# Old keys and values of the sample attention: regrouped within DRAM ahead of the mixer, then loaded in 4 KB rows

## The chip, the cores and the metric

One Trainium2 chip, one of its cores. The metric is the device time of one execution in microseconds; lower is better. The kernel before takes 2782.64 us (median of 3 runs, 2779.88 to 2784.14).

## What is computed

One inference step of one decoder layer over 256 prompt tokens and 64 sample tokens (8 sequences of 8), 320 columns in all: a SwiGLU feed-forward, a token mixer (mLSTM and dilated attention), a second feed-forward, a final norm. For the change, one part of the mixer matters: the dilated attention of the sample tokens over a cache of 2048 old keys and values for each of the 8 sequences, 8 heads of 128 numbers each, so that a row of the cache is 1024 fp32 numbers (4 KB).

```python
PATTERNS = ((128, 1), (512, 4), (2048, 16))       # window, dilation

def dilated_attention_sample(q, k_all, v_all, biases):
    qi = k_all.shape[1] - T + jnp.arange(T)        # T = 8 new tokens
    for (w, d), bias in zip(PATTERNS, biases):
        idx = qi[:, None] - d * jnp.arange(w // d + 1)[None, :]
        kg = k_all[:, idc]                         # idc = clip(idx, 0)
        vg = v_all[:, idc]
        s = jnp.einsum('bthe,btjhe->bhtj', q, kg) + bias
        ...
        num = jnp.einsum('bhtj,btjhe->bthe', p, vg)
```

Beyond the last 512 positions only the third pattern is left, dilation 16: of the 1536 far rows, 8 in each group of 16 neighbours are read (one for each of the 8 new tokens), 768 rows for each sequence.

## The kernel before

Every large product is written out in one list of jobs, each with its weights in chunks of 512 x 256 fp32 numbers (512 KB). For a chunk the SyncE queue (SP) loads a `raw` buffer (5 of them), ScalarE casts it to `hi` (L225), VectorE subtracts `lo` (L226), and TensorE runs 24 matmuls (L144) of 320 columns, which give fp32 accuracy from two rounded halves. `run_job` goes from chunk to chunk; ahead of the matmuls of chunk i it splits up to chunk i + 2, steps the side work once, and issues loads up to chunk i + 7. The order of every engine is thus the order in which the program is written. The job list is feed-forward a (272 chunks), the mixer's input projection, gates, the mixer's output projections, feed-forward b.

The side work is written as generators that advance by one `yield` per chunk (`every`), per second chunk (`even`, `odd`), or eight times in fifteen chunks (`slow`). In the first part of the projection runs `sample_attention` (`slow`): 16 units, each one sequence b and four heads hg. For a unit, `load_k` brings its keys in five pieces pr into `kraw` (3 buffers) and `load_v` its values in six pieces pc into `vt` (6 buffers). Pieces 0 and 1 of each are the 512 near rows, with a DMA of 512 KB each. The others are far rows: `kraw` pieces 2 to 4 hold 256 of them in 128 partitions, two rows to a partition, `vt` pieces 2 to 5 hold 192 in 96. For four heads, half of a cache row is wanted, 2 KB; the two halves of such a buffer (index g) are filled by two DMAs of 128 or 96 rows of 2 KB. VectorE then transposes each `kraw` (L654), in line with its `lo` of the weights; TensorE takes `vt` directly. In the same stretch run the mLSTM (`odd`), which loads and stores its matrix state C, and `prompt_attention`, and most intermediate results go to DRAM and come back, all on the SP queue, in the order of the program (L141 is the helper that issues nearly every DMA). A DMA also waits until the eighth before it has landed, since the tracked semaphores are used in turn.

Of the kernel before, what the change touches and what calls it, by code (L numbers as in the profile page):

```python
# [9 lines left out]
F32 = mybir.dt.float32  # L10
# [12 lines left out]
PAST = 2048  # L23
# [105 lines left out]
def decoder_kernel(tc, I, O, K):  # L129
# [7 lines left out]
    dp = es.enter_context(tc.tile_pool(name="dp", bufs=1, space=DRAM))  # L137
    es.enter_context(tc.manual_schedule())

    def dma(out, in_):  # L140
        nc.sync.dma_start(out, in_)  # L141

    def mm(out, a, b, start=True, stop=True, **kw):
        T.matmul(out, a, b, start=start, stop=stop, **kw)  # L144

    def bcast(ap, n, at=1):
        shape = list(ap.shape)
        shape.insert(at, n)
        idx = [slice(None)] * len(ap.shape)
        idx.insert(at, None)  # L150
        return ap[tuple(idx)].to_broadcast(shape)

    def raw_ap(ap, off, dims):
        return bass.AP(tensor=ap.tensor, offset=ap.offset + off, ap=dims)
# [3 lines left out]
    def later(fn, n=1):  # L158
        later_q.append([n, fn])
# [23 lines left out]
    def spawn(g, lst=None, first=False):  # L183
        lst = every if lst is None else lst
        lst.insert(0 if first else len(lst), g)
# [68 lines left out]
    def bg_tile():  # L254
        return pp.tile([128, 512], F32, tag="bg", bufs=4, name="bg")
# [79 lines left out]
    def tr(out, in_):  # L335
        k = in_.shape[0]
        T.transpose(out, in_, ident[:k, :k])  # L337
# [14 lines left out]
    rows_d = dp.tile([4, 2, NT], F32, name="rows_d")  # L352
    sc_d = dp.tile([4, 2 * NS], F32, name="sc_d")
    sT_d = dp.tile([1, 32], F32, name="sT_d")

    XH, XL = {}, {}

# [73 lines left out]
    def load_vecs():  # L431
        for r, nm in ((16, "ln_mix"), (32, "ln_ffb"), (48, "conv_b")):
            dma(vrow[r - 16:r, 0], I[nm].rearrange("o (k p) -> (o k) p", p=128))
        dma(vrow[48:112, 0], I["conv_w"].rearrange("o i (k p) -> (o i k) p", p=128))
        dma(vrow[0:8, 1], I["m_norm"].rearrange("o (k p) -> (o k) p", p=128))
        dma(vrow[8:24, 1], I["ln_f"].rearrange("(k p) -> k p", p=128))
# [72 lines left out]
    def mxt(shape, tag, bufs, name, dt=F32):  # L509
        return M["p"].tile(shape, dt, tag=tag, bufs=bufs, name=name)  # L510
# [119 lines left out]
    def sample_attention():  # L630
        ck, cv = I["cache_k"][0], I["cache_v"][0]
# [9 lines left out]
        def load_k(u, pr):  # L641
            hg, b = divmod(u, 8)
            t = mxt([128, 2, 512], "kr", KRB, "kraw")
            off = b * PAST * 1024 + hg * 512
            if pr < 2:
                dma(t, raw_ap(ck, off + (1536 + 2 * pr) * 1024, [[4096, 128], [1024, 2], [1, 512]]))
            else:
                for g in range(2):
                    dma(t[:, g], raw_ap(ck, off + 16 * (2 * (pr - 2) + g) * 1024, [[96 * 1024, 16], [1024, 8], [1, 512]]))
            kraw[u, pr] = t  # L650

        def tk(u, pr):
# [5 lines left out]
        def load_v(u, pc):  # L658
            hg, b = divmod(u, 8)
            t = mxt([128, 2, 512], "v4", 6, "vt")  # L660
            off = b * PAST * 1024 + hg * 512
            if pc < 2:
                dma(t, raw_ap(cv, off + (1536 + 256 * pc) * 1024, [[1024, 128], [128 * 1024, 2], [1, 512]]))
            else:
                hf, gp = divmod(pc - 2, 2)
                for g in range(2):
                    dma(t[0:96, g], raw_ap(cv, off + 16 * (48 * gp + 24 * g + 12 * hf) * 1024,
                                           [[16 * 1024, 12], [1024, 8], [1, 512]]))
                if pc == 4:
                    dma(t[96:104, 0], vs_d[8 * b:8 * b + 8, hg * 512:(hg + 1) * 512])  # L670
            VT[u, pc] = t
# [14 lines left out]
        for pr in range(KRB):  # L686
            load_k(0, pr)
        yield
        for pr in range(5):
            tk(0, pr)  # L690
            load_k(*divmod(pr + KRB, 5))
            yield
# [782 lines left out]
    def last_tr(m):  # L1475
        xn, a = Y["xn"], bg_tile()
        for t, t0 in enumerate(TOK):
            tr(a[:, t * 128:(t + 1) * 128], xn[:, m, t0:t0 + 128])
        return a
# [87 lines left out]
    def first_chunk(n, ps):  # L1567
# [18 lines left out]
        wh.pop(n)  # L1586
        wl.pop(n)

    def vec_table():
        for _ in range(8):  # L1590
            yield
        load_vecs()
        for _ in range(4):
            yield
        vps = bg_tile()
        tr(vps[:, 0:112], vrow[0:112, 0])
        tr(vps[:, 112:136], vrow[0:24, 1])
        V.tensor_copy(gv[:, 16:152], vps[:, 0:136])

    def first_sumsq():  # L1600
        for c in ((), (), (), (0, 1), (2, 3), (4, 5, 6, 7)):
            for j in c:
                sumsq(X[j], j, fp)
            yield

    def init_tables():
        for _ in range(6):
            yield
        tab = fp.tile([128, TABW], F32, name="tab")
        dma(tab, K["tab"])  # L1610
        rel = fp.tile([128, 8], F32, name="rel")
        for u in range(4):
            dma(rel[32 * u:32 * u + 32], I["rel_table"])
        cst = fp.tile([24, D], F32, name="cst")
        dma(cst, I["state_conv"].rearrange("o b r c -> (o b r) c"))
        n0 = fp.tile([64, 128], F32, name="n0")
        dma(n0, I["state_n"].rearrange("o b h (k p) -> (o b h k) p", p=128))
        for _ in range(6):
            yield
        lt = fp.tile([128, 2, 3, 128], F32, name="lt")  # L1620
        for hg in range(2):
            rb = bcast(rel[:, 4 * hg:4 * hg + 4], 32, 2)
            for kt in range(3):
                G.tensor_tensor(lt[:, hg, kt].rearrange("p (h c) -> p h c", h=4), rb,
                                bcast(tab[:, T_DL + 32 * kt:T_DL + 32 * kt + 32], 4), op=OP.mult)
        sr = fp.tile([8, RW], F32, name="sr")
        ps, pb = bg_tile(), bg_tile()
        for c0, q in ((0, ps), (RW // 2, pb)):
            mm(q[0:8, 0:RW // 2], rel[0:32], tab[0:32, T_OHR + c0:T_OHR + c0 + RW // 2])
            V.tensor_copy(sr[:, c0:c0 + RW // 2], q[0:8, 0:RW // 2])  # L1630
        yield
        dma(srev_d, sr)
        yield
        yield
        sb = fp.tile([128, 2, 128], F32, name="sb")
        for t in range(8):
            for hg in range(2):
                dma(sb[t:128:8, hg], raw_ap(srev_d[:], 4 * hg * RW + 7 - t, [[RW, 4], [128, 4], [1, 128]]))
            yield
        for hg in range(2):  # L1640
            ps = bg_tile()
            mm(ps[:, 128:320], lt[:, hg, 0], tab[:, T_OHO:T_OHO + 192])
            for kt in range(2):
                mm(ps[:, 320:328], lt[:, hg, 1 + kt], tab[:, T_OHN + 8 * kt:T_OHN + 8 * kt + 8], kt == 0, kt == 1)
            V.tensor_tensor(ttab[:, hg, 0:128], sb[:, hg], tab[:, T_MK:T_MK + 128], op=OP.add)
            V.tensor_tensor(ttab[:, hg, 128:SCOLS], ps[:, 128:SCOLS], tab[:, T_MK + 128:T_MK + SCOLS], op=OP.add)
            yield
        ps = bg_tile()
        mm(ps[0:8, 0:384], rel[0:32], tab[0:32, T_OHP:T_OHP + 384])
        gs = fp.tile([8, 384], F32, name="gs")  # L1650
        V.tensor_tensor(gs, ps[0:8, 0:384], tab[0:8, T_MKP:T_MKP + 384], op=OP.add)
        yield
        dma(grev_d, gs)
        flip = fp.tile([128, 128], F32, name="flip")
        dma(flip, K["flip"])
        ps = bg_tile()
        for k in range(16):
            tr(ps[:, 24 * k:24 * k + 24], cst[:, k * 128:(k + 1) * 128])
        V.tensor_copy(convst, ps[:, 0:384].rearrange("p (k c) -> p k c", k=16))
        yield  # L1660
        ps = bg_tile()
        tr(ps[:, 0:64], n0)
        V.tensor_copy(n0T, ps[:, 0:64])
        for p in range(4):
            tw = fp.tile([128, 3, 512], F32, tag="xl", bufs=3, name="tw")
            tf, to = tw[:, 0], tw[:, 1]
            dma(tf.rearrange("p (a c) -> p a c", a=2), raw_ap(grev_d[:], 2 * p * 384, [[1, 128], [384, 2], [1, 256]]))
            yield
            ps = bg_tile()
            mm(ps, flip, tf)  # L1670
            V.tensor_copy(to, ps)
            later(lambda to=to, p=p: dma(tp_d[p], to), 2)

    spawn(first_sumsq())
    spawn(vec_table())
    spawn(init_tables(), even)
    for job in jobs[:-1]:
        run_job(job)
# [5 lines left out]
    a = last_tr(1)  # L1684
# [56 lines left out]
```

## Time and profile before

| | |
|---|---|
| median of 3 runs | 2782.64 us |
| the profiled execution | 2780.48 us, of it 2778.7 us span |
| TensorE busy | 2727.4 us, 98% of the span |
| VectorE, ScalarE busy | 1534.0 us, 1104.3 us |
| DMA | 557.22 MB, 201 GB/s over the span |
| mean granted TensorE clock | 0.993 |

The span is the time from the first instruction to the last. Feed-forward a runs from 60 to 897 us, the projection with the attention and the mLSTM beside it to about 1630, the gates and output projections to 1903, feed-forward b to the end.

### The profile page before, as it was taken

The page shows a single profiled execution, that of the slowest core. Times are in us where ns is not written, and L with a number is a line of the kernel's source. Part 1 is how long each engine was busy: PE and PEld are TensorE (multiplying, and loading weights), DVE is VectorE, ACT ScalarE, POOL GpSimd, SP SyncE. Part 2 cuts the span into 40 slices and gives each one's busy share as a digit, 9 for nine tenths or more (in the row PEclk, how much of TensorE's full clock was granted, in tenths as well). Part 3 has the DMA queues.
Part 4 walks back from the last instruction along what each step waited for, and adds up shares of the span by engine and source line. Part 5 has one row for each costly group of instructions (what it writes and reads, how often), then busy time and mean ns, then how long its engine had stood idle before and what let it go on. Part 6 is the DMA issues. An engine that isn't in the chain of part 4 may idle for free.

```text
span 2778.7 us, 51128 instructions
## 1 busy us (share of the span) xinstructions
PE 2727.4 (98%) x21522; PEld 2678.3 (96%) x21522; DVE 1534.0 (55%) x1815; ACT 1104.3 (40%) x1379; POOL 179.5 (6%) x226
## 2 busy tenths in 40 slices
PE   9999999999999999998999999999999999999998
PEld 8999999999999999987989899999999999999998
DVE  6444444444447656776766565755444444444444
ACT  5333333333335333544543434544333333333344
POOL 0100000000000000111211100000000000000000
PEclk9999999999999999999999999999999999999999
DMA  6555555555556789999999997655555555545543
GB/s 213 163 160 179 160 162 164 160 157 163 166 155 206 213 218 301 288 290 265 308 307 304 320 302 251 205 184 170 161 164 159 163 160 167 159 152 174 160 152 114
DMA packets 507763, 557.22 MB, mean 201 GB/s; under 512 B 30156, under 2 KB 452604, under 8 KB 507508
## 3 DMA queue, kind: packets, MB, share of 16 engines
q1 hardware_dynamic: 506828, 552.43, 65.4%
q8 instruction: 168, 2.75, 0.4%
q10 hardware_dynamic: 704, 1.52, 0.2%
q14 instruction: 63, 0.52, 0.1%
HBM read 521.58 MB, written 32.28 MB: 199 GB/s over the span
## 4 chain that ended last, share of the span: by engine, by line
PE 86%; DMA 9%; DVE 3%; ACT 1%; issue 1%; POOLq 0%; POOL 0%; SPq 0%; ACTq 0%; DVEq 0%
PE fg L144 82%; DMA raw<-in_w_in_dram 4%; PE bg L144 3%; DMA kraw<-in_cache_k_dram 2%; PE bg L337 1%; DVE lo L226 1%; DMA vt<-in_cache_v_dram 1%; ACT hi L225 0%; DVE kd L654 0%; DMA out_C_sample_dram<-C 0%; DMA vh<-vm_d 0%; DMA out_conv_sample_dram<-cs 0%; DVE y L947 0%; DMA vq<-vm_d 0%; DMA mo_d<-sg 0%
## 5 line engine op out<-in xcount | busy, mean ns | idle before, releaser
L226 DVE TENSOR_TENSOR lo<-raw,hi 128x1024 fp32r<-128x1024 f32 (+1 forms) x780 | 956.9, 1234 | 894.0 <-ACT hi L225 876.9
L144 PE MATMUL fg<-xh,hi 128*128 128x320 f32 x4240 | 1277.6, 302 | 1.7 <-ACT hi L225 1.6
L144 PE MATMUL fg<-xh,lo 128*128 128x320 f32 x4240 | 1267.8, 300 | 10.9 <-DVE lo L226 10.9
L144 PE MATMUL fg<-xl,hi 128*128 128x320 f32 x4240 | 1267.3, 300 | 0.0
L225 ACT CAST hi<-raw 128x1024 fp32r<-128x1024 f32 (+1 forms) x780 | 796.8, 1027 | 1092.4 <-PE fg L144 912.0
L144 PEld LDWEIGHTS fg<-xh,lo 128*128 128x128 f32 x4240 | 802.1, 189 | 12.9 <-DVE lo L226 12.8
L144 PEld LDWEIGHTS fg<-xh,hi 128*128 128x128 f32 x4240 | 802.3, 190 | 4.1 <-ACT hi L225 2.1
L144 PEld LDWEIGHTS fg<-xl,hi 128*128 128x128 f32 x4240 | 802.4, 190 | 0.7
L144 PE MATMUL fg<-hh,hi 128*128 128x320 f32 x1408 | 423.7, 301 | 0.0
L144 PE MATMUL fg<-hl,hi 128*128 128x320 f32 x1408 | 421.0, 299 | 0.0
L144 PE MATMUL fg<-hh,lo 128*128 128x320 f32 x1408 | 421.0, 299 | 0.0
L144 PEld LDWEIGHTS fg<-hh,hi 128*128 128x128 f32 x1408 | 266.1, 189 | 1.7 <-issue 1.6
L144 PEld LDWEIGHTS fg<-hl,hi 128*128 128x128 f32 x1408 | 266.1, 189 | 1.0 <-issue 1.0
L144 PEld LDWEIGHTS fg<-hh,lo 128*128 128x128 f32 x1408 | 266.1, 189 | 0.0
L464 POOL TENSOR_TENSOR gt<-gt,rstd 128x640 f32<-128x640 f32 x44 | 68.3, 1552 | 1788.8 <-ACT gt L463 1788.8
L144 PE MATMUL fg<-bh,hi 128*128 128x320 f32 x512 | 153.3, 299 | 0.0
L144 PE MATMUL fg<-bl,hi 128*128 128x320 f32 x512 | 153.1, 299 | 0.0
L144 PE MATMUL fg<-bh,lo 128*128 128x320 f32 x512 | 153.1, 299 | 0.0
L654 DVE STREAM_TRANSPOSE kd<-kraw 128x1024 f32<-128x1024 f32 x80 | 96.5, 1220 | 32.5 <-DMA kraw<-in_cache_k_dram 32.5
L144 PEld LDWEIGHTS fg<-bh,hi 128*128 128x128 f32 x512 | 96.8, 189 | 0.2 <-issue 0.2
L144 PEld LDWEIGHTS fg<-bl,hi 128*128 128x128 f32 x512 | 96.8, 189 | 0.0
L144 PEld LDWEIGHTS fg<-bh,lo 128*128 128x128 f32 x512 | 96.8, 189 | 0.0
(301 smaller groups left out, 1375.7 us busy)
## 6 DMA issues: line engine op xcount, KB each, us to landing
raw<-in_w_in_dram SPq DMA_DIRECT2D x176, 512.0 KB
raw<-in_w_ffb_in_dram SPq DMA_DIRECT2D x176, 512.0 KB
raw<-in_w_ffa_in_dram SPq DMA_DIRECT2D x175, 512.0 KB
raw<-in_w_ffa_out_dram SPq DMA_DIRECT2D x80, 512.0 KB
raw<-in_w_ffb_out_dram SPq DMA_DIRECT2D x80, 512.0 KB
kraw<-in_cache_k_dram SPq DMA_DIRECT2D x96, 256.0 KB
vt<-in_cache_v_dram SPq DMA_DIRECT2D x128, 192.0 KB
kraw<-in_cache_k_dram SPq DMA_DIRECT2D x32, 512.0 KB
```

The source lines that it names most:

```text
L144: T.matmul(out, a, b, start=start, stop=stop, **kw)
L225: S.copy(hi[:, :nk], t[:, :nk])
L226: V.tensor_tensor(lo[:, :nk], t[:, :nk], hi[:, :nk].bitcast(F32), op=OP.subtract)
L337: T.transpose(out, in_, ident[:k, :k])
L464: G.tensor_tensor(gt, gt, bcast(rstd, 2), op=OP.mult)
L654: V.transpose(kd[:, 2 * pr:2 * pr + 2].rearrange("p a b -> p (a b)"), t.rearrange("p a b -> p (a b)"))
```

## The change

During feed-forward a, a new generator `gather_old` copies the far rows of all units from the cache into two new sets of DRAM tensors, `fk_d` and `fv_d`, one DMA for each chunk: 16 units with 6 copies of keys (128 rows of 2 KB) and 8 of values (96 rows), 224 copies. It skips its first ten steps. In the copy, the two rows that share a partition stand side by side. In the mixer, each far piece is one DMA with 4 KB for each partition instead of two with 2 KB: 112 loads where 224 were. Arithmetic, buffers and the near loads are as before.

```diff
+    fk_d = [dp.tile([3, 128, 1024], F32, name=f"fk_d{u}") for u in range(16)]
+    fv_d = [dp.tile([4, 96, 1024], F32, name=f"fv_d{u}") for u in range(16)]
...
@@ load_k
-                for g in range(2):
-                    dma(t[:, g], raw_ap(ck, off + 16 * (2 * (pr - 2) + g) * 1024, [[96 * 1024, 16], [1024, 8], [1, 512]]))
+                dma(t, fk_d[u][pr - 2].rearrange("p (a c) -> p a c", a=2))
...
@@ load_v
-                hf, gp = divmod(pc - 2, 2)
-                for g in range(2):
-                    dma(t[0:96, g], raw_ap(cv, off + 16 * (48 * gp + 24 * g + 12 * hf) * 1024,
-                                           [[16 * 1024, 12], [1024, 8], [1, 512]]))
+                dma(t[0:96], fv_d[u][pc - 2].rearrange("p (a c) -> p a c", a=2))
...
+    def gather_old():
+        ck, cv = I["cache_k"][0], I["cache_v"][0]
+        for _ in range(10):
+            yield
+        for u in range(16):
+            hg, b = divmod(u, 8)
+            off = b * PAST * 1024 + hg * 512
+            for i in range(3):
+                for g in range(2):
+                    dma(fk_d[u][i].rearrange("(x r) (g c) -> x r g c", r=8, g=2)[:, :, g],
+                        raw_ap(ck, off + 16 * (2 * i + g) * 1024, [[96 * 1024, 16], [1024, 8], [1, 512]]))
+                    yield
+            for i in range(4):
+                hf, gp = divmod(i, 2)
+                for g in range(2):
+                    dma(fv_d[u][i].rearrange("(x r) (g c) -> x r g c", r=8, g=2)[:, :, g],
+                        raw_ap(cv, off + 16 * (48 * gp + 24 * g + 12 * hf) * 1024, [[16 * 1024, 12], [1024, 8], [1, 512]]))
+                    yield
...
     spawn(vec_table())
+    spawn(gather_old())
```

TensorE, VectorE, ScalarE and GpSimd execute the same instructions in the same order before and after. Only the SP queue changes, in two stretches. The first is feed-forward a, near its twentieth chunk: loads of constants (`cst`, `n`), then loads of weights (`raw`). On SP stood there:

```order
L141 DMA cst<-in_state_conv_dram 24x2048
L141 DMA n_729<-in_state_n_dram 64x128
L141 DMA raw<-in_w_ffa_in_dram 128x4x256 x14
L141 DMA srev_d<-sr 8x520
L141 DMA raw<-in_w_ffa_in_dram 128x4x256 x4
```

And now stand there, with the copies of the first unit's keys (`fk_d_96`):

```order
L141 DMA cst<-in_state_conv_dram 24x2048
L141 DMA n_763<-in_state_n_dram 64x128
L141 DMA fk_d_96<-in_cache_k_dram 128x1x512
L141 DMA raw<-in_w_ffa_in_dram 128x4x256
L141 DMA fk_d_96<-in_cache_k_dram 128x1x512
L141 DMA raw<-in_w_ffa_in_dram 128x4x256
```

Each load of weights has one copy ahead of it, from the eleventh step to the 234th of the 272 of this feed-forward.

The second stretch is the mixer. In the eighth unit of the attention, far values (`vt`) stand on SP between weights, results of the mLSTM (`out_C_prompt`, `out_C_sample`) and near keys, as a piece of the difference:

```order
 L141 DMA raw<-in_w_in_dram 128x4x256
 L141 DMA out_C_prompt_dram<-cn 128x2x256
-L141 DMA vt<-in_cache_v_dram 96x1x512 x2
-L141 DMA raw<-in_w_in_dram 128x4x256
-L141 DMA vt<-in_cache_v_dram 96x1x512 x2
+L141 DMA vt<-fv_d_119 96x1024
+L141 DMA raw<-in_w_in_dram 128x4x256
+L141 DMA vt<-fv_d_119 96x1024
 L141 DMA out_C_sample_dram<-C 128x2x256
 L141 DMA kraw<-in_cache_k_dram 128x2x512
```

Two loads of 2 KB rows became one of 4 KB rows, in the same place. A few rows later on SP the same is seen with far keys (`kraw`):

```order
 L141 DMA raw<-in_w_in_dram 128x4x256
 L141 DMA out_C_sample_dram<-C 128x2x256
-L141 DMA kraw<-in_cache_k_dram 128x1x512 x2
+L141 DMA kraw<-fk_d_105 128x1024
 L141 DMA raw<-in_w_in_dram 128x4x256 x2
 L141 DMA out_C_sample_dram<-C 128x2x256
```

Nothing but the pair moved; the weights behind it stand one issue nearer.

## Rows read from the trace of the kernel before

**Rows 1.** Page, busy time by engine; then TensorE and DMA in 40 slices.

```profile
PE 2727.4 (98%) x21522; PEld 2678.3 (96%) x21522; DVE 1534.0 (55%) x1815; ACT 1104.3 (40%) x1379; POOL 179.5 (6%) x226
...
DMA  6555555555556789999999997655555555545543
```

**Rows 2.** Windows by stage: stretch, its length, busy time, granted clock, DMA share, GB/s.

```profile
core 0: us, PE busy (x) PEld busy (x) DVE busy (x) ACT busy (x) POOL busy (x), PEclk, DMA share, GB/s
60.00:770.00 710.00, 710.00 (x5206) 705.73 (x5205) 341.39 (x312) 249.84 (x256) 33.54 (x25) 1.00 0.54 165
1000.00:1200.00 200.00, 197.01 (x1913) 189.89 (x1911) 136.11 (x242) 80.79 (x139) 17.68 (x30) 1.00 1.00 282
1200.00:1300.00 100.00, 92.65 (x900) 85.11 (x901) 71.81 (x125) 44.48 (x69) 19.16 (x38) 0.97 0.94 277
1300.00:1400.00 100.00, 90.20 (x834) 83.25 (x833) 68.87 (x116) 52.48 (x80) 20.11 (x29) 0.95 1.02 303
1400.00:1500.00 100.00, 93.95 (x868) 86.53 (x867) 69.62 (x102) 42.48 (x68) 17.49 (x33) 0.97 1.02 312
1500.00:1630.00 130.00, 124.03 (x1200) 116.28 (x1199) 82.89 (x122) 49.70 (x76) 19.84 (x27) 0.97 1.02 310
1630.00:1903.00 273.00, 273.00 (x2182) 270.94 (x2181) 163.41 (x181) 124.63 (x152) 0.00 (x0) 1.00 0.69 220
```

**Rows 3.** Waits, 1000 to 1630 us: who waited for whom, us, times, longest.

```profile
ACT hi L225 <- DMA raw<-in_w_in_dram: 59.7, 15, 9.0
DVE kd L654 <- DMA kraw<-in_cache_k_dram: 32.5, 9, 7.9
PE fg L144 <- DVE lo L226: 9.5, 4, 5.5
PE bg L144 <- DVE lo L226: 6.4, 1, 6.4
PE bg L144 <- DMA vh<-vm_d: 6.0, 1, 6.0
```

**Rows 4.** Chain that ended last, 1260 to 1345 us: start, us, what.

```profile
1257.52 9.15 DMA kraw<-in_cache_k_dram
...
1273.93 12.44 DMA raw<-in_w_in_dram
```

**Rows 5.** Waits of the SP queue itself, 1000 to 1630 us; then 232 to 897 us.

```profile
SPq L141 <- DMA raw<-in_w_in_dram: 108.9, 85, 2.9
SPq L141 <- DMA vt<-in_cache_v_dram: 48.8, 90, 1.8
SPq L141 <- DMA kraw<-in_cache_k_dram: 27.2, 51, 1.8
...
SPq L141 <- DVE lo L226: 566.3, 211, 5.0
```

**Rows 6.** Page, issues of far keys and of far values: count, KB each.

```profile
kraw<-in_cache_k_dram SPq DMA_DIRECT2D x96, 256.0 KB
vt<-in_cache_v_dram SPq DMA_DIRECT2D x128, 192.0 KB
```

**Rows 7.** DMA, 300 to 500 us, weights alone: packets, MB, share of 16 engines.

```profile
DMA packets 32401, 32.37 MB, mean 162 GB/s; under 512 B 992, under 2 KB 32386, under 8 KB 32386
q1 hardware_dynamic: 32386, 32.15, 52.2%
```

**Rows 8.** DMA, 938 to 939 us, while near keys arrive.

```profile
DMA packets 234, 0.41 MB, mean 406 GB/s; under 512 B 13, under 2 KB 59, under 8 KB 234
q1 hardware_dynamic: 234, 0.41, 105.8%
```

**Rows 9.** DMA, 1000 to 1630 us.

```profile
DMA packets 147805, 185.77 MB, mean 295 GB/s; under 512 B 12531, under 2 KB 105662, under 8 KB 147740
q1 hardware_dynamic: 147740, 184.87, 99.5%
```

**Rows 10.** DMA, 2771 to 2778.7 us: the output, stored with 4 KB a packet.

```profile
DMA packets 594, 2.07 MB, mean 269 GB/s; under 512 B 89, under 2 KB 89, under 8 KB 594
q1 hardware_dynamic: 313, 1.05, 47.3%
q10 hardware_dynamic: 281, 1.02, 34.3%
```

**Rows 11.** SP's issues: `kraw`, `vt` overall; `raw` 232 to 897 us (ns min/median/max).

```profile
L141 SPq DMA_DIRECT2D kraw<-in_cache_k_dram x128: 367/582/1381, 908.3 to 1632.7; - x128
L141 SPq DMA_DIRECT2D vt<-in_cache_v_dram x160: 368/810/2170, 1006.4 to 1677.8; - x160
L141 SPq DMA_DIRECT2D raw<-in_w_ffa_in_dram x128: 367/368/368, 244.8 to 804.0; - x128
```

## Prediction

> **What bounds the kernel now.** First the page: TensorE is busy 98% of the span, and the DMA row stands at five or six tenths except in one stretch in the middle, where it stands at nine [rows 1]. So I asked for windows by stage [rows 2]. In feed-forward a (60 to 770 us) TensorE has no idle microsecond and DMA is 0.54 busy; from 1630 on TensorE is full again. Between lies the only place where time is lost: 2.99 us idle in 1000 to 1200, then 7.35, 9.80, 6.05 and 5.97 us in the four windows to 1630, together 32.2 us. In the same four windows the granted clock falls to 0.95 to 0.97, which costs up to 0.03 x 100 + 0.05 x 100 + 0.03 x 100 + 0.03 x 130 = 15 us more; part of the low clock lies inside the idle time, so I count 12. The ceiling for a change that acts on the mixer alone is thus about 44 us, 1.6% of the whole, and since TensorE is full behind it, what is won there moves the end by as much.
>
> What makes TensorE wait? In that stretch all 16 DMA engines are busy (0.94 to 1.02). The waits [rows 3] show the way it takes: VectorE stands 32.5 us before the transposes of `kraw`, ScalarE 59.7 us before casts of `raw`, and TensorE then waits for `lo`, which stands behind these in VectorE's order (9.5 + 6.4 us), or for a DMA itself. The chain agrees [rows 4]: links of 9 and 12 us from the issue of a load to its landing. The SP queue shows the backlog from the other side: 108.9 + 48.8 + 27.2 = 185 us it waits for the landing of earlier DMAs, while in feed-forward a it waits for `lo` alone, which means for a free buffer [rows 5]. So the mixer is bound by DMA, or near it; feed-forward a is bound by TensorE with DMA to spare.
>
> **What the far loads cost, and what they will.** There are 96 loads of 128 rows and 128 loads of 96 rows [rows 6], 12,288 + 12,288 = 24,576 packets of 2 KB, between 1006 and 1678 us [rows 11]. The price of a packet comes from stretches with known mixtures. Weights alone: 52.2% of 16 engines over 200 us is 1670 us for 32,386 packets, 51.6 ns for 1 KB [rows 7]. Near keys in a quiet microsecond: 16.9 us of engine time, less 46 packets of 1 KB, leaves 14.5 us for 175 packets, 83 ns for 2 KB [rows 8]. In the mixer: 99.5% of 16 x 630 is 10,030 us; 93,131 packets of 1 KB take 4,806 of it, 12,531 small ones between nothing and 650, so the 42,078 of 2 KB and a little more take 109 to 124 ns each [rows 9]. I take 117. The far loads then hold the 16 engines for 24,576 x 0.117 / 16 = 180 us.
>
> After the change there are 12,288 packets of 4 KB. No row shows such a load. The nearest are the stores of the output: 281 packets of the second queue in 34.3% of 7.7 us, 42.3 us, of which 249 would be 4 KB, 170 ns; both queues together 100.5 us for 505 packets, 199 ns [rows 10]. From below stand two quiet packets of 2 KB, 166 ns; from above two of the mixer's, 234 ns, which would be no gain. I take 180, near the stores, because the new rows are contiguous as theirs are: 12,288 x 0.180 / 16 = 138 us. The gain is 42 us of DMA time over the 672 us, 6.2% (0 at 234 ns; 9% at 166 against 124).
>
> Half the issues of far loads go too: 48 of `kraw` at a median 0.58 us and 64 of `vt` at 0.81 us, 80 us of SP's time in the mixer [rows 11]. SP is in order, so weights that stand behind a pair are issued sooner; and each DMA that SP waits for is larger, so that the same number in flight covers more bytes. I give this no sum of its own: it is what could turn the 6.2% into more.
>
> What it gives TensorE: from 1200 to 1630 the stage goes at the pace of DMA, so 6.2% of 430 us is 27 us, of 29 us idle and 12 us of clock lost there. In 1000 to 1200 only 3 us are lost, and I count 1 of it. Sum: 28 us.
>
> **What the copies cost in feed-forward a.** A step there is 24 of 5206 matmuls in 710 us, 3.27 us [rows 2]. The weights of a step are 512 packets, 32 for each engine, 32 x 51.6 ns = 1.65 us; 1.62 us are left. A copy adds 128 or 96 packets, on average (6 x 8 + 8 x 6) / 14 = 6.9 for each engine. No row shows a copy from DRAM to DRAM. Bounds: as cheap as a quiet load, 83 ns; as dear as two of the mixer's packets one after the other, 234 ns. Between them I take a quiet read and a quiet write in turn, 166 ns, since feed-forward a is nearer to the quiet rows than to the mixer: 1.14 us, and the step needs 2.79 of 3.27 us. It breaks even at 1.62 / 6.9 = 235 ns, just at the upper bound. The cover is five `raw` buffers and idle DMA; if it is gone, each 10 ns beyond costs 0.069 x 224 = 15 us, and the next thing late is `raw` for the cast, then TensorE. SP has room for 224 more issues: it waits 566 of 665 us for buffers [rows 5], and an issue takes 0.37 us [rows 11]. A copy waits for nothing but the landing of the eighth DMA before it, four steps ago, and the weights behind it in the queue wait for a buffer anyway. The last copy is issued some 38 steps, 120 us, before the mixer reads the first, so that the new dependence costs nothing. I cost feed-forward a at nothing.
>
> [...]
>
> **Sum.** 2780.5 us of the profiled execution, less 28, is 2752.5. That execution is 2.1 us under the median of the runs, 2782.6; with half of that I say 2753.
>
> **Rivals.** *Full relief* (chance 0.18): fewer issues and larger DMAs in flight do more than the share says, or 4 KB costs 166 ns. For it speak the 185 us that SP waits for landings; against it, that some loads stand behind others' results (`vh` from `vm_d`), which keep their way through DRAM. 2780 - 40 = 2740.
>
> *The row size buys nothing* (0.14): a packet costs by its bytes, 4 KB is 2 x 117, and TensorE's waits come from bursts rather than the mean. For it speaks that quiet prices are proportional beyond a few ns (83 for 2 KB, 170 for 4 KB), so all the gain lies in the mixer's surcharge of 34 ns, which I cannot tie to the far rows; in 1000 to 1200 DMA stands at 1.00 and TensorE loses only 1.5%. Then 2775 to 2786. [...]
>
> *Feed-forward a becomes bound by DMA* (0.22): a copy reads and writes the same DRAM from which the weights stream, and a packet passes 235 ns. At 270 ns: 0.035 x 6.9 x 224 = 54 us lost, 28 won, 2806; at 300 ns 2852. For it speaks that the upper bound is already at break-even; against it, that DMA is idle 46% of that time and that a single copy stands between weights, never two.
>
> **Chances and range.** The forecast, 15 to 36 us less, has 0.46; full relief 0.18, nothing 0.14, the loss 0.22. The two first make it faster, and a little of the third: 0.66. Within 0.2% (5.6 us, about what a measurement of this kernel can tell from no change): 0.14. Slower: 0.20. Its own range is 2744 to 2768; since cases of both signs hold much, I give 2738 to 2804, which leaves out the far end of the loss and a gain near the ceiling.
>
> **What would show it.** Right: feed-forward a keeps TensorE at 100% with a DMA share near 0.8; in 1200 to 1630 the share falls under 1.00 or the stage becomes shorter by some 27 us; the waits of VectorE for `kraw` shrink most; packets of 4 KB cost 170 to 190 ns. Wrong: idle TensorE behind `lo` between 60 and 770 us, with SP waiting there for landings rather than for `lo`; or an unchanged wait for `raw` and `kraw` in the mixer although DMA has become less busy, which would mean that bursts and order, not the mean load, set it.

## The result and the profile after

The changed kernel takes 2747.25 us (median of 4 runs, 2745.51 to 2749.30), beside 2781.57 us of the kernel before (median of 4 runs here, the profiled one among them): 34.3 us less, and a ratio of 0.9886 (95% interval 0.9871 to 0.9900). The forecast was 2753 us, within 2738 to 2804.

The profiled execution took 2745.51 us, its span 2743.7. The windows of the changed kernel by stage, with the columns of [rows 2]; the mixer's part that had ended at 1630 us now ends at about 1595:

```profile
core 0: us, PE busy (x) PEld busy (x) DVE busy (x) ACT busy (x) POOL busy (x), PEclk, DMA share, GB/s
60.00:770.00 710.00, 710.00 (x5206) 705.73 (x5205) 341.35 (x312) 250.12 (x256) 33.53 (x25) 1.00 0.74 234
1000.00:1200.00 200.00, 200.00 (x1977) 192.78 (x1976) 141.21 (x260) 82.61 (x141) 17.39 (x30) 1.00 1.00 296
1200.00:1300.00 100.00, 94.94 (x886) 88.38 (x885) 76.44 (x128) 52.59 (x81) 19.76 (x38) 0.97 0.95 294
1300.00:1400.00 100.00, 96.50 (x916) 90.56 (x916) 81.05 (x128) 52.90 (x83) 26.64 (x41) 1.00 1.03 331
1400.00:1500.00 100.00, 98.89 (x928) 92.62 (x927) 68.52 (x97) 44.47 (x69) 17.62 (x28) 1.00 1.05 333
1500.00:1600.00 100.00, 100.00 (x1042) 93.42 (x1041) 66.11 (x96) 41.16 (x63) 14.73 (x18) 1.00 1.02 322
...
1595.00:1870.00 275.00, 275.00 (x2196) 272.83 (x2195) 164.61 (x182) 126.76 (x153) 0.00 (x0) 1.00 0.70 220
```

Three things are to be seen. Feed-forward a is exactly as full as it was (5206 matmuls, no idle time), with DMA at 0.74 instead of 0.54: the copies are hidden. In the mixer, TensorE's idle time falls from 32.2 us to 5.06 + 3.50 + 1.11 = 9.7 us, and the clock is below full in one window where it was in four. But DMA is no less busy: its share is 0.95 to 1.05 where it was 0.94 to 1.02. What has changed is what the engines move in that time, 322 to 333 GB/s from 1300 us on where 303 to 312 had been. They were not relieved; they became faster.

The waits of the changed kernel from 1000 to 1630 us, beside [rows 3]:

```profile
ACT hi L225 <- DMA raw<-in_w_in_dram: 23.8, 7, 5.6
DVE kd L655 <- DMA kraw<-fk_d: 10.5, 4, 3.7
...
PE bg L144 <- DMA vh<-vm_d: 4.7, 1, 4.7
...
PE fg L144 <- DVE lo L226: 2.1, 1, 2.1
```

VectorE waits 10.5 us for keys where it waited 32.5, ScalarE 23.8 for weights where it waited 59.7, and TensorE 2.1 for `lo` where it waited 9.5 + 6.4. And SP, in the same stretch, beside [rows 5]:

```profile
SPq L141 <- DVE lo L226: 85.5, 53, 5.1
SPq L141 <- DMA raw<-in_w_in_dram: 70.9, 74, 2.4
SPq L141 <- DMA vt<-fv_d: 28.0, 38, 1.5
```

Before, it had waited less for buffers:

```profile
SPq L141 <- DVE lo L226: 27.0, 25, 3.3
```

It is now held by buffers (`lo`, 85.5 us) more than by any one kind of landing, though landings of weights, values and keys together still hold it for 135 us (185 before).

### The profile page after: what moved, and what is told of

It reads as the page before. It is cut to its first block, busy times and chain, and to the rows that moved or that the text cites. A ratio compares the mean times of both kernels' runs of the same rounds, so it can differ in the third digit from the quotient of the medians.

```text
span 2743.7 us, 51211 instructions
## 1 busy us (share of the span) xinstructions
PE 2715.4 (99%) x21522; PEld 2670.7 (97%) x21522; DVE 1533.7 (56%) x1815; ACT 1105.5 (40%) x1379; POOL 181.3 (7%) x226
## 2 busy tenths in 40 slices
DMA packets 521843, 607.56 MB, mean 221 GB/s; under 512 B 31948, under 2 KB 454396, under 8 KB 521588
## 4 chain that ended last, share of the span: by engine, by line
PE 50%; ACT 0%; POOLq 0%; POOL 0%; DVE 0%; issue 0%
PE fg L144 47%; PE bg L144 3%; PE bg L337 0%; POOLq L1755 0%; POOL Y L1719 0%; ACT hi L225 0%; ACT L1196 0%; ACT xn L1450 0%; DVE x L1445 0%; ACT sq L392 0%; DVE lo L226 0%; ACT re L1196 0%; DVE x L1469 0%; ACT sq L1470 0%; ACT rt L1704 0%
## 5 line engine op out<-in xcount | busy, mean ns | idle before, releaser
L655 DVE STREAM_TRANSPOSE kd<-kraw 128x1024 f32<-128x1024 f32 x80 | 96.3, 1218 | 10.5 <-DMA kraw<-fk_d 10.5
```

Source lines behind the costliest of these rows:

```text
L655: V.transpose(kd[:, 2 * pr:2 * pr + 2].rearrange("p a b -> p (a b)"), t.rearrange("p a b -> p (a b)"))
```

## The experiments

The change does several things at once to a far piece: one load instead of two, rows of 4 KB instead of 2 KB, other addresses, and perhaps another number of engines that work at a load. The last, called the spread over the engines below, is an assumption of mine about the loads of values, whose source is in 12 groups in the cache and in adjacent rows in the copy; no trace here gives a packet's engine. Each experiment changes one of these, or as few as can be parted. All times are medians (of 4 runs, or of 10 where the time came near that of before); the ratio, with its 95% interval, is to the kernel before on the same chip, whose median was 2778.4 to 2779.9 us there. Engine time below is the time that packets took, summed over the 16 DMA engines.

**Two loads of 2 KB rows, from the copies.** Number of loads and row size go back; the copies and their addresses stay.

```diff
-                dma(t, fk_d[u][pr - 2].rearrange("p (a c) -> p a c", a=2))
+                for g in range(2):
+                    dma(t[:, g], fk_d[u][pr - 2][:, g * 512:(g + 1) * 512])
```

The same for `vt` with `fv_d`. Expected:

> The copies stay; each far piece is again loaded by two DMAs of 2 KB rows, now from the copied tensors, where the rows lie close together. Three theories of the 34 us that were won. Row size or number of loads (one load of 4 KB rows where two of 2 KB were): it takes nearly all of it back, 2775 to 2782 us. [...] Place of the rows (scattered in the cache, close together in the copy): the gain stays as well.

Measured: 2745.98 us, ratio 0.9872 (0.9846 to 0.9899). The whole gain is there. My theory of row size falls, and the number of loads with it; the layout and the spread over the engines are left.

**One load, 2 KB packets.** The copies are laid out in two blocks, so that one DMA has two runs of 2 KB for each partition.

```diff
-    fk_d = [dp.tile([3, 128, 1024], F32, name=f"fk_d{u}") for u in range(16)]
+    fk_d = [dp.tile([3, 2, 128, 512], F32, name=f"fk_d{u}") for u in range(16)]
...
-                dma(t, fk_d[u][pr - 2].rearrange("p (a c) -> p a c", a=2))
+                dma(t, fk_d[u][pr - 2].rearrange("g p c -> p g c"))
```

> The copies stay, in an order in which the two rows of a partition lie in two blocks; each far piece is one DMA with two runs of 2 KB for each partition. Number of loads: the gain stays, 2745 to 2752 us. Row size (the packet of 4 KB is cheaper than two of 2 KB): the gain is lost, 2770 to 2782. Spread over the engines, or place of the rows: the gain stays. Together with the kernel of two loads it parts number from row size.

Measured: 2746.02 us, ratio 0.9877 (0.9852 to 0.9903). The DMA view from 1000 to 1590 us shows why, first of this kernel and then of the changed one:

```profile
DMA packets 145162, 183.68 MB, mean 311 GB/s; under 512 B 11313, under 2 KB 103504, under 8 KB 145098
q1 hardware_dynamic: 145098, 182.79, 101.5%
```

```profile
DMA packets 135197, 184.73 MB, mean 313 GB/s; under 512 B 11367, under 2 KB 104065, under 8 KB 135132
q1 hardware_dynamic: 135132, 183.83, 100.6%
```

Ten thousand packets fewer, and nearly the same engine time for nearly the same bytes: 101.5% of 16 x 590 us is 9582 us for 182.79 MB, 52.4 us per MB; the changed kernel needs 9497 us for 183.83 MB, 51.7. A packet of 4 KB costs about as much as two of 2 KB. The times of single packets in the two traces say the same: in this stretch one of 4 KB took 222 ns on average in the changed kernel, one of 2 KB 108 ns in this one, near rows among them.

**The copies alone.** `gather_old` runs, and the mixer loads from the cache as before.

> The copies are made, but the mixer loads from the cache as before, two DMAs of 2 KB for each piece. If the copies are hidden as the trace of the changed kernel says (TensorE full from 60 to 770 us), this is the time of before, 2778 to 2785 us. If they cost something that the mixer's gain has covered, it is slower than before by that much.

Measured: 2778.98 us, ratio 0.9997 (0.9980 to 1.0014). The copies cost nothing that this interval could tell, and it is the loads that won.

**Values in 12 groups.** The copied values get a gap behind each group of eight rows, so that their outermost count is 12 again. The question is whether the gain stays.

```diff
-    fv_d = [dp.tile([4, 96, 1024], F32, name=f"fv_d{u}") for u in range(16)]
+    fv_d = [dp.tile([4, 12, 9, 1024], F32, name=f"fv_d{u}") for u in range(16)]
...
-                dma(t[0:96], fv_d[u][pc - 2].rearrange("p (a c) -> p a c", a=2))
+                dma(t[0:96], fv_d[u][pc - 2][:, 0:8].rearrange("x r (a c) -> x r a c", a=2))
```

> As the changed kernel, but the copied values lie in 12 groups of 8 rows with a gap of one row behind each group, so that the outermost count of the load's source is 12, as it was in the cache; still one load of 4 KB rows for each piece. [...] Row size, number of loads or place of rows: it stays, 2745 to 2752.

Measured: 2760.81 us, ratio 0.9925 (0.9899 to 0.9951). The page's line on packets, of this kernel and of the changed one:

```profile
DMA packets 521587, 607.55 MB, mean 221 GB/s; under 512 B 31692, under 2 KB 454140, under 8 KB 521332
```

```profile
DMA packets 521843, 607.56 MB, mean 221 GB/s; under 512 B 31948, under 2 KB 454396, under 8 KB 521588
```

256 packets under 512 B fewer: 4 for each of the 64 loads. I read this as four engines fewer, which no trace shows. About 14 us of the gain go with the 12 groups and their gap, 18 stay. Something else came along: one of these loads takes SP at least 760 ns to issue, where it took 314 from the copy without gaps.

```profile
L141 SPq DMA_DIRECT2D vt<-fv_d x64: 760/804/2622, 1006.3 to 1653.5; - x64
```

At this point the spread over engines looked like a good part of the answer. The next two runs took that back.

**Values alone, and keys alone.** Only one of the two is copied and loaded in one DMA; the other is loaded from the cache as before.

> [...] Place of the rows (or any theory in which each byte of far rows counts alike): keys are half of the bytes, so half the gain goes, 2760 to 2768.

Measured: 2781.38 us, ratio 1.0004 (0.9989 to 1.0019). Nothing is won, where the place of the rows, by bytes, had half the gain.

> [...] Place of the rows, by bytes: half the gain, 2760 to 2768. [...]

Measured: 2752.09 us, ratio 0.9892 (0.9863 to 0.9920). Nearly everything is won, more than the half that the place of the rows, by bytes, had. So the 18 us that stayed with the values in 12 groups belonged to the keys; the values count at most when the keys are mended, and then by a few microseconds that these intervals do not tell from none (0.9892 against 0.9877 and 0.9886). The values alone also clear SP's time: their 64 loads go out at a median of 0.470 us each, where all 160 loads from the cache, 128 of them far, went at 0.810 [rows 11], and that bought nothing.

```profile
L141 SPq DMA_DIRECT2D vt<-fv_d x64: 314/470/2086, 1006.5 to 1677.3; - x64
```

Summed over the trace, SP spends 143 us on issuing all `kraw` and `vt` in the kernel with values alone and 166 us in the one with keys alone (206 us before); the second is 29 us faster. SP's time is not what was won.

**12 groups, two loads.** The values with the gap, and two loads of 2 KB rows for every piece, keys and values; with one load it was 2760.81 us.

> [...] Place of the rows: 2757 to 2765 as well. [...]

Measured: 2754.53 us, ratio 0.9898 (0.9875 to 0.9921). Two loads are not slower than one with 12 groups either. The two runs put the price of 12 groups at 8 to 14 us against the kernels with the values adjacent, with intervals that touch or overlap (keys alone, whose values come in 12 groups from the cache, lie 5 us behind); it is a price of the groups, the gap and the longer issue together, and these runs do not part them.

**The outermost count of another load.** The mLSTM's `vq`, whose source has 4 outermost, by four DMAs of 32 rows where two of 128 rows were, for each head.

```diff
-            for g in range(2):
-                dma(vq[:, g * 256:(g + 1) * 256], raw_ap(vm_d[:], (SEQ + 32 * g) * 1024 + h * 256,
-                                                        [[0, 4], [1024, 32], [1, 256]]))
+            for r in range(4):
+                dma(vq[32 * r:32 * r + 32].rearrange("p (g c) -> p g c", g=2),
+                    raw_ap(vm_d[:], SEQ * 1024 + h * 256, [[1024, 32], [32 * 1024, 2], [1, 256]]))
```

> [...] If these loads are too few to count, 2744 to 2750, and the 8 added issues cost nothing to speak of.

Measured: 2748.44 us, ratio 0.9877 (0.9853 to 0.9901): no more than the changed kernel has. The loads did change: the page's packets under 512 B rise from 31,948 to 32,172, by 224, which fits 16 loads with 16 of them each in place of 8 with 4.

**Where the keys' rows lie.** In the cache, a load of far keys reads 16 groups of eight rows, the groups 384 KB apart; in the copy, 128 rows that follow each other (2 KB of every 4 KB, in a group as in the copy, when a piece is loaded by two DMAs). Three kernels copy only the keys and load each piece by two DMAs of 2 KB rows as before. They differ in the layout of the copy alone: that of the cache (the diff below), the same with groups 388 KB apart (`KP` is 97), and close together (a tile of its own for each piece).

```diff
+    KP = 96
+    fk_d = [dp.tile([16, KP, 1024], F32, name=f"fk_d{b}") for b in range(8)]
...
+                for g in range(2):
+                    n = 16 * (2 * (pr - 2) + g)
+                    dma(t[:, g], fk_d[b][:, n:n + 8, hg * 512:hg * 512 + 512])
```

> Far keys alone are copied, into tensors with the layout of the cache: 16 groups 96 rows (384 KB) apart, so that each of the two loads of 2 KB rows of a piece reads the same pattern of addresses as before, only elsewhere. Pattern of the keys' addresses (16 regions 384 KB apart read at once): nothing is won, 2775 to 2783 us. Anything else that the copy does (a tensor of its own, rows lately written): the gain stays, 2748 to 2757.

Measured: 2783.19 us, ratio 1.0020 (1.0005 to 1.0034). Nothing is won; if anything it is a little slower.

> As the kernel with the cache's layout, but the groups are 97 rows (388 KB) apart; the rows lie as far from each other as before. [...] If it is that the rows lie in many places at all: nothing is won, 2775 to 2783.

Measured: 2779.04 us, ratio 1.0001 (0.9986 to 1.0015).

> Far keys alone are copied, close together, and loaded by two DMAs of 2 KB rows as before: the reference for the two kernels with wider layouts, from which it differs in the layout alone. If neither number nor row size counts for the keys, it is the kernel with the keys alone in one load: 2748 to 2757 us. If they count, it lies between that and before, 2760 to 2775.

Measured: 2752.80 us, ratio 0.9911 (0.9885 to 0.9938). The DMA view from 1000 to 1590 us, of the kernel with 388 KB and of the one with the rows close together:

```profile
DMA packets 137639, 172.25 MB, mean 292 GB/s; under 512 B 11941, under 2 KB 98818, under 8 KB 137578
q1 hardware_dynamic: 137578, 171.41, 99.4%
```

```profile
DMA packets 145939, 183.30 MB, mean 311 GB/s; under 512 B 12421, under 2 KB 104311, under 8 KB 145875
q1 hardware_dynamic: 145875, 182.42, 98.5%
```

Both keep all engines busy; the first moves 292 GB/s, the second 311. In engine time, 99.4% of 16 x 590 us for 171.41 MB is 54.7 us per MB, against 51.0. The issue on SP shows it as well, in the same order of kernels:

```profile
L141 SPq DMA_DIRECT2D kraw<-fk_d x96: 520/572/1147, 908.6 to 1640.5; - x96
```

```profile
L141 SPq DMA_DIRECT2D kraw<-fk_d x96: 319/378/1496, 908.2 to 1600.3; - x96
```

A load with 16 groups takes SP 572 ns to issue at the median, one of adjacent rows 378. What follows: the gain belongs to the layout of the keys' rows in DRAM. Having a tensor of its own, or rows lately written, is not it (384 KB); that one distance is not it (388 KB). From 1000 to 1590 us all kernels fall into two groups by this layout alone: with the keys in 16 distant groups (before, copies alone, values alone, 384 KB, 388 KB) the stage moves 292 to 294 GB/s at 54.3 to 56.3 us of engine time per MB; in all others, with the keys close together, it moves 306 to 314 GB/s at 50.8 to 52.4. Within a group the engine time does not order the kernels: values alone have the 56.3, and the time of before with its 54.3.

**Near keys too.** The changed kernel with 32 more copies, of the near keys, and their loads in 4 KB rows.

```diff
-                dma(t, raw_ap(ck, off + (1536 + 2 * pr) * 1024, [[4096, 128], [1024, 2], [1, 512]]))
+                dma(t, nk_d[u][pr].rearrange("p (a c) -> p a c", a=2))
...
+            for i in range(2):
+                dma(nk_d[u][i].rearrange("p (a c) -> p a c", a=2),
+                    raw_ap(ck, off + (1536 + 2 * i) * 1024, [[4096, 128], [1024, 2], [1, 512]]))
+                yield
```

> The changed kernel with the near keys copied as well (32 more copies of 256 rows in feed-forward a), and loaded with 4 KB rows. [...] Pattern of addresses: some of the 10 us of idle time that are left goes, 2738 to 2745 us. If the far keys were all: 2744 to 2750. DMA in feed-forward a rises from 0.74 to about 0.80, which stays hidden.

Measured: 2744.62 us, ratio 0.9875 (0.9854 to 0.9895), within the interval of the changed kernel. Its windows:

```profile
60.00:770.00 710.00, 710.00 (x5206) 705.95 (x5206) 341.02 (x312) 250.11 (x257) 33.45 (x25) 1.00 0.77 246
1000.00:1200.00 200.00, 200.00 (x1977) 192.78 (x1976) 141.02 (x260) 82.72 (x141) 16.16 (x30) 1.00 0.98 294
1200.00:1630.00 430.00, 422.10 (x4103) 395.92 (x4103) 308.95 (x472) 202.91 (x311) 80.31 (x125) 1.00 1.01 320
```

TensorE is idle 7.9 us where the changed kernel had 9.7 from 1200 to 1630. It may be 1 to 3 us better; these runs do not tell.

## Why the prediction was right, and where it was not

**Where the time was lost, and the ceiling: right.** The 34.3 us came out of the mixer: 22.5 us of it was idle TensorE, the rest goes to the lower clock by the forecast's reckoning, and the end moved by as much. The way from a late load over VectorE to `lo` shrank. It was not the waits for `kraw` that shrank most, as the prediction had it, but those for `raw`: 35.9 us of ScalarE's against 22.0 of VectorE's (60% and 68% of what they had been). The weights came sooner too, not the keys alone.

**The price of a row of 4 KB: wrong.** The step "I take 180, near the stores" failed. From a copy whose rows are adjacent, one load of 4 KB rows and two of 2 KB rows take the same time (2747.25, 2745.98 and 2746.02 us), and engine time per MB is within 1.5%. In the traces from 1000 to 1590 us a packet of 4 KB took 222 ns on average, and two of 2 KB in the kernels with the same copies 212 (two loads) and 216 (one load), near rows among them. With 222 for 180 the far loads would hold the engines for 170 us after 180, and the prediction's sum would have won some 6 us of TensorE's time in place of 27. Twice a packet of 2 KB was the true price, and the rival *the row size buys nothing* was right about the mechanism. It was wrong about the time, as I was right about the time with the wrong mechanism: the 6.2% less engine time that I derived from packets is close to the 6.8% per MB (54.7 to 51.0) that came from where the keys' rows lie. That agreement is luck. The prediction's own sign shows it: "packets of 4 KB cost 170 to 190 ns" did not come. What it had not seen is that the surcharge of 34 ns on a packet of 2 KB, which it "cannot tie to the far rows", is in part tied to them. By the packets of the traces, one of 2 KB (far and near) took 114 ns on average with the keys in 16 distant groups (388 KB) and 103 with them close together, where a quiet one takes 84; a packet of weights (1 KB) fell from 56 to 53 beside it. So some third of the surcharge belongs to the far keys' layout, and the rest stays.

**Fewer issues, more bytes in flight: no effect seen.** The term that I gave no sum deserved none. SP's time for issuing `kraw` and `vt` did fall by 82 us (206 to 123, the forecast was 80), but half the issues for values alone bought nothing; all issues, but close rows, had the whole gain (2745.98 us), and keys alone with all theirs won 25 us. SP's waits for landings thus look like a sign of slow DMA rather than its cause.

**The copies cost nothing: right, by a wide margin.** The DMA view from 60 to 770 us prices them, first of the kernel before and then of the changed one:

```profile
q1 hardware_dynamic: 116286, 116.36, 53.3%
```

```profile
DMA packets 143456, 166.49 MB, mean 234 GB/s; under 512 B 6979, under 2 KB 118642, under 8 KB 143379
q1 hardware_dynamic: 143403, 165.73, 73.2%
```

The copies took the difference of 19.9% of 16 x 710 us, 2261 us. They moved the difference of 49.4 MB, some 24,100 packets of 2 KB, so 94 ns each at most; the packets of 2 KB themselves took 89 ns on average. I had taken 166, a read and a write in turn; the measured price is near a quiet load alone, 83 ns, my lower bound. A step then needs 1.65 + 6.9 x 0.094 = 2.3 of 3.27 us, and the rival of a feed-forward bound by DMA was never near: break-even lay at 235 ns. In that price nothing is seen of the far keys' pattern, although the copies read it too: from 60 to 770 us packets of 2 KB took 89 ns on average with keys alone copied and 90 with values alone. There a copy stands alone between weights and DMA is 0.64 busy.

**The spread over the engines: not shown.** The loads of values in 12 groups have 4 packets under 512 B less each than those of adjacent rows (31,692 against 31,948 in all, for 64 loads); how many engines worked at them no trace tells. The values alone, whose loads go from 12 groups to adjacent rows, won nothing (2781.38 us).

**What stays open.** Why loads from 16 groups are dear. The layouts with 384 and 388 KB differ from the close one in distance and in the form of the access at once (16 x 8 rows against 128 rows); keys in groups with a small gap, which would part the two, were not tried. Some runs give hints and no more. Values in 12 groups 36 KB apart did not raise the engine time per MB, 52.0 and 51.2 us against 51.7 and 51.9 with the values adjacent. Near keys, whose pairs of rows lie 16 KB apart, gained 3 us at most from a copy. And the copies, which read the same distant groups with DMA not full, were not dear. The far values also come in groups, 12 of them 64 KB apart, and gave nothing alone; whether their loads are not dear, or were only hidden behind dear keys, these runs do not say. Why the keys' loads slow everything around them is seen (GB/s, engine time per MB) but not explained.

## What to carry to other kernels

When all DMA engines are busy and the consumer waits, look at the bytes moved rather than the share: a share near 1.00 stood at 292 and at 311 GB/s, and the difference was the layout of one eighth of the bytes (79 loads of 256 KB in 171 MB). A stage with idle DMA could reorder data for a later one here at nearly the price of a load (94 ns a packet of 2 KB at most, beside 83), and a copy for copying's sake, with the old loads behind it, tells in one run whether that is free. Before believing a mechanism that gave the right number, take its parts one at a time: here row size, number of loads and the spread over the engines each had a good story, and none of them had the main part of the gain.

## What the runs showed of the hardware that was not expected

In feed-forward a of the changed kernel, a copy from DRAM to DRAM of 2 KB rows cost a packet 94 ns at most, near a quiet load's 83. In the mixer, a packet of 4 KB cost about what two of 2 KB cost (222 against 212 and 216 ns). A load of 128 rows in 16 groups took SP 520 ns at least to issue, one of 128 adjacent rows 319, and one of 96 rows in 12 groups 760 where adjacent ones took 314. With the far keys in 16 distant groups the mixer's DMA, which was full, needed about 7% more engine time per MB (54.7 against 51.0 us). A distance of 384 KB between the groups was dear (2783.19 us, against 2752.80 with the rows close together), and 4 KB more did not cure it (2779.04 us).
